# Two-layer conditioned trunk: another order inside the groups of seven products, and of the first loads, copies and splits

## The chip, the cores and the metric

The kernel runs on one core of a Trainium2 chip. The metric is device microseconds (us) of one execution. Engines are named as in the profile: PE is the matmul engine (PEld its weight loads), DVE the vector engine, ACT the scalar engine, POOL GpSimd, SP the engine that issues most DMAs.

## What is computed

The reference is a decoder trunk of two layers on 512 tokens of width 1024, in fp32. Each layer has three sub-layers, each with a normalisation that is scaled and shifted by values made from a conditioning vector c:

```python
cs = jax.nn.silu(c)
for l in range(DEPTH):
    mod = (cs @ ada_w[l] + ada_b[l])          # 3 sub-layers x (shift, scale, gate)
    h = _rmsnorm(x, norm_g[l, 0]) * (1.0 + mod[:, 0, 1]) + mod[:, 0, 0]
    x = x + 0.5 * mod[:, 0, 2] * _swiglu(h, ffn_w_gate[l, 0], ffn_w_up[l, 0], ffn_w_down[l, 0])
    h = _rmsnorm(x, norm_g[l, 1]) * (1.0 + mod[:, 1, 1]) + mod[:, 1, 0]
    x = x + mod[:, 1, 2] * _mixer(h, w_in[l], conv_w[l], w_conv_out[l], w_attn_out[l], w_o[l], rel_bias)
    h = _rmsnorm(x, norm_g[l, 2]) * (1.0 + mod[:, 2, 1]) + mod[:, 2, 0]
    x = x + 0.5 * mod[:, 2, 2] * _swiglu(h, ffn_w_gate[l, 1], ffn_w_up[l, 1], ffn_w_down[l, 1])
return _rmsnorm(x, final_g)
```

`_swiglu` is `(silu(h @ w_gate) * (h @ w_up)) @ w_down` with an inner width of 2816 (22 blocks of 128); `_mixer` is a short convolution beside dilated window attention. So there are four FFNs and two mixers, in the order FFN, mixer, FFN, FFN, mixer, FFN.

## The kernel before, in words

**Numbers.** Every matmul operand is split into a high and a low part (`A.copy` on ACT makes the high one, `sub`, L145, on DVE the low one), and each product is three matmuls: high x high, high x low, low x high. The activations stay transposed on chip: `xT` (the residual), and `hh` and `hl`, the two parts of the modulated, normalised input of a sub-layer, in eight blocks k of 128 features by 512 tokens.

**Where things lie.** Split operands lie in a pool R of 49 slots, fp32 scratch in a pool F of 19 slots (128x512 each). `Slots.take` hands out the first slot in the list of free ones; a slot that is given back goes to the list's end. Who takes a slot waits until its last readers are done. The PSUM banks have three tags: "mm" (4), "at" (2), "o" (2).

**An FFN.** Gate and up weights are multiplied in groups of two blocks of 128 columns (`m`, `m + 1`). One group is `seven`: a 2x2 block product by seven products instead of eight. a and c are the two halves of the gate weights (by input features), b and d those of the up weights. The products need a, c as loaded, or the differences a-b, a-d, b-d, c-a (L558, on DVE), against a quarter of `h` (`quarter`) or one of four sums of quarters (`Sums`, once for each FFN: four additions or subtractions of 128x1024 and four splits). Each product has 24 matmuls of 128x256. Its results are copied out of PSUM (`kept`, L554, on ACT) and added up (`plus`, L561, on DVE). After two or three groups the matching part of the down product runs (`down`, L214 splits its weights), and adds to `xT` (L373).

**Between sub-layers** stands `boundary`: `finish` computes the last part of the down product in two token halves; for each half the norm is summed up (`Norm`), and `modulated` makes `hh` and `hl` block by block: `t` = xT times the norm (L361, DVE), then `hh` (L362, ACT), an fp32 copy `u` (L366 on ACT for even k, L364 on POOL for odd k), then `hl` (L145, DVE). `t` lies in a slot that is taken and given back for each k. Behind each k stand 12 matmuls of 128x256, of the first four weight blocks of the next sub-layer.

**Modulation.** `modulation` loads 512 KB of `ada_t` for each k (SP), and multiplies and sums it against c on DVE (L297); these steps are spread over the products (`tick`). In the FFNs two loads are ahead, in the mixers one (`depth=1`).

**The start.** x is loaded and transposed by PE into PSUM, copied to `xT` (L1211 on ACT, L1213 on DVE), the first weights are split (L214; the first parts on POOL), c is loaded by ACT's queue, and the first FFN's `hh` and `hl` are made block by block while PE multiplies them (L1268).

**What sets the order.** The program is written as one sequence; a scheduler reorders the instructions of each engine by its own cost model, and each engine then works through its list in order, waiting at semaphores.

Of the kernel before, what the change touches and what calls it, by code (L numbers as in the profile page):

```python
# [27 lines left out]
ALU = mybir.AluOpType  # L28
# [18 lines left out]
N_R, N_LOW, N_F, RAWS = 49, 33, 19, 4  # L47
# [29 lines left out]
class Slots:  # L77
# [38 lines left out]
def trunk(ctx: ExitStack, tc: tile.TileContext, x, c, ada_t, ada_b, norm_g, ffn_w_gate, ffn_w_up, ffn_w_down,  # L116
# [196 lines left out]
    def modulation(l, s, j, depth=2):  # L313
# [10 lines left out]
        for k in range(depth):  # L324
            fetch(k)
        for k in range(NC):
            w = ahead.pop(0)
            weighted(m, k, w.ap)
            w.give()
            fetch(k + depth)  # L330
            yield
# [120 lines left out]
    def boundary(src, rhs, gate, l, s, units, whole=None):  # L452
# [14 lines left out]
        finish(src, rhs, gate, norms, hook)  # L467
        dsts = [bank("mm") for _ in units]
# [12 lines left out]
        return dsts  # L481
# [55 lines left out]
    def seven(raw1, raw2, sums, done):  # L537


        a, c = raw1[:, :4], raw1[:, 4:]  # L540
        b, d = raw2[:, :4], raw2[:, 4:]

        def run(*args):
            p = product(*args)
            next(p)
            return p

        def end(p):
            for _ in p:
                pass  # L550

        def kept(src):
            s = F.take()
            A.copy(s.ap, src)  # L554
            return s

        def minus(dst, x, y):
            V.tensor_tensor(dst, x, y, op=ALU.subtract)  # L558

        def plus(s, src):  # L560
            V.tensor_tensor(s.ap, s.ap, src, op=ALU.add)  # L561

        one = bank("mm")
        end(run(a, quarter(0, 0), one, True))
        p1 = kept(one)
        yield
        minus(a, b, a)
        three = bank("o")
        p = run(a, sums(1), three, True)
        minus(a, d, a)  # L570
        end(p)
        end(run(a, sums(2), one))
        u2 = kept(one)
        two = bank("at")
        end(run(c, quarter(1, 0), two, True))
        plus(p1, two)
        minus(b, d, b)
        end(run(b, sums(3), one))
        u3 = kept(one)
        plus(u3, three)  # L580
        yield
        minus(c, c, a)
        end(run(c, quarter(1, 1), one))
        end(run(d, sums(4), three))
        plus(u2, three)
        done(p1, u2, one, u3)

# [30 lines left out]
    def ffn(l, i, get, first, whole):  # L618

        acts = {}  # L620
        R.top = N_LOW
        sums = Sums(whole.ap.rearrange("p (k n) -> p k n", k=NC))
        whole.give()

# [10 lines left out]
        def swiglu_pair(m):  # L635
            def done(g1, u1, g2, u2):

                A.activation(g1.ap, g1.ap, AF.Silu)
                V.tensor_tensor(u1.ap, u1.ap, g1.ap, op=ALU.mult)
                g1.give()  # L640
                s = F.take()
                A.activation(s.ap, g2, AF.Silu)
                V.tensor_tensor(u2.ap, u2.ap, s.ap, op=ALU.mult)
                s.give()
                hi, lo = R.take(2), R.take(2)
                hv, lv = (s.ap.rearrange("p (c n) -> p c n", c=2) for s in (hi, lo))
                for half, t in enumerate((u1, u2)):
                    tv = t.ap.rearrange("p (c n) -> p c n", c=2)
                    A.copy(hv[:, :, HALF[half]], tv)  # L649
                    sub(lv[:, :, HALF[half]], tv, f(hv[:, :, HALF[half]]))  # L650
                    t.give()
                acts[m], acts[m + 1] = zip(hi.apart(), lo.apart())

            return done

        ahead = {}

        def begin(m):

            if m < DFF // P:  # L660
                ahead[m] = seven(*get.raws(m), sums, swiglu_pair(m))
                next(ahead[m])

        def up(part):
            modulating["share"] = SHARE_UP
            for m in range(*part):
                if m in acts:
                    continue
                if m < len(first) or m % 2:
                    if m < len(first):  # L670
                        pg, pu = first[m]
                    else:
                        g, u = get(m)
                        pg, pu = any_bank(), any_bank()
                        project([(pg, g)], h, NC)
                        project([(pu, u)], h, NC)
                    swiglu(m, pg, pu)
                    if m % 2 and m + 1 >= len(first):
                        begin(m + 1)
                    continue  # L680
                pair = ahead.pop(m)
                next(pair)
                begin(m + 2)
                for _ in pair:
                    pass
                if m + 2 == DFF // P:
                    sums.give()
# [478 lines left out]

    cs = F.take(2)
# [211 lines left out]
```

## Time and profile before

| what | us |
|---|---|
| median of 3 runs (2685.22 to 2687.23) | 2686.24 |
| the profiled execution | 2685.69 |
| its span, first to last instruction | 2683.9 |
| PE busy in it | 2620.5 (98%) |
| DVE busy | 1838.3 (68%) |
| ACT busy | 1171.6 (44%) |

The profiled execution is 0.55 us under the median. A matmul's row shows its own length; matmuls overlap, so what one costs is the distance from its start to the next one's. The mean granted clock of PE is 0.993 of full speed.

### The profile page before, as it was taken

Reading aid. Unit: us, or ns where it says so; the run is one execution under the profiler, and the core shown is the slowest. Engines: PE = TensorE matmul, PEld = TensorE weight load, DVE = VectorE, ACT = ScalarE, POOL = GpSimd, SP = SyncE. Lnnn points to the kernel's source line nnn. Section 1 sums busy time; section 2 is a strip of 40 time slices with the busy share of each in tenths; the row PEclk is TensorE's granted clock in tenths of the full one; section 3 lists DMA queues with packets and bytes.
Section 4 is the critical chain, followed back from the end, with each engine's and each line's share of the span. In section 5 each row is a group of like instructions: output and inputs, shape, how many; then the busy total and the mean of one; then the engine's idle time right before and its main releaser. Section 6 shows DMA issues by size and latency. Waiting matters only on the chain.

```text
span 2683.9 us, 40526 instructions
## 1 busy us (share of the span) xinstructions
PE 2620.5 (98%) x16265; PEld 2347.2 (87%) x16265; DVE 1838.3 (68%) x2874; ACT 1171.6 (44%) x2200; POOL 227.7 (8%) x551
## 2 busy tenths in 40 slices
PE   6899999999999999999999999999999999999999
PEld 5798999788888889989999999988888888989998
DVE  7996778888463358667787777885536534677675
ACT  4453454343353236434554444543443423544443
POOL 1000023121010001000020000330110000200001
PEclk8999999999999999999999999999999999999999
DMA  8732246767222231333224332562322322133321
GB/s 282 249 128 91 93 146 222 270 203 248 75 95 79 87 118 44 99 110 109 96 64 130 106 110 77 179 217 86 97 69 79 118 81 85 63 111 99 98 83 67
DMA packets 285480, 326.42 MB, mean 122 GB/s; under 512 B 8057, under 2 KB 263404, under 8 KB 285292
## 3 DMA queue, kind: packets, MB, share of 16 engines
q1 hardware_dynamic: 284836, 323.19, 36.8%
q8 instruction: 127, 2.08, 0.3%
q10 hardware_dynamic: 456, 0.65, 0.1%
q14 instruction: 61, 0.50, 0.1%
HBM read 321.67 MB, written 2.13 MB: 121 GB/s over the span
## 4 chain that ended last, share of the span: by engine, by line
PE 84%; DVE 9%; DMA 3%; ACT 3%; issue 1%; POOL 1%; DVEq 0%; POOLq 0%; SPq 0%; ACTq 0%
PE mm L531 16%; PE mm L234 12%; PE mm L235 12%; PE mm L236 12%; PE o L531 8%; PE at L531 4%; PE mm L1046 3%; DMA slots_f<-in_ada_t_dram 2%; DVE slots_f L297 2%; PE o L234 2%; PE o L236 2%; PE o L235 2%; PE at L236 2%; PE at L234 2%; PE at L235 2%; DVE slots_r L145 2%
## 5 line engine op out<-in xcount | busy, mean ns | idle before, releaser
L214 DVE TENSOR_TENSOR slots_r<-raw,slots_r 128x512 fp32r<-128x512 f32 (+2 forms) x578 | 361.0, 642 | 340.5 <-PE mm L235 162.1
L213 ACT CAST slots_r<-raw 128x512 fp32r<-128x512 f32 (+2 forms) x584 | 325.1, 582 | 403.2 <-PE mm L236 170.9
L234 PE MATMUL mm<-hh,slots_r 128*128 128x512 f32 (+1 forms) x1320 | 487.8, 370 | 0.0
L235 PE MATMUL mm<-hl,slots_r 128*128 128x512 f32 (+1 forms) x1320 | 483.0, 366 | 0.0
L236 PE MATMUL mm<-hh,slots_r 128*128 128x512 f32 (+1 forms) x1320 | 482.2, 365 | 0.0
L145 DVE TENSOR_TENSOR slots_r<-raw,slots_r 128x1024 fp32r<-128x1024 f32 (+3 forms) x401 | 379.9, 970 | 130.2 <-ACT slots_r L522 55.4
L522 ACT CAST slots_r<-raw 128x1024 fp32r<-128x1024 f32 x273 | 282.5, 1048 | 363.0 <-DVE raw L558 93.7
L236 PEld LDWEIGHTS mm<-hh,slots_r 128*128 128x128 f32 x1320 | 248.4, 188 | 43.3
L234 PEld LDWEIGHTS mm<-hh,slots_r 128*128 128x128 f32 x1320 | 248.9, 189 | 36.5
L235 PEld LDWEIGHTS mm<-hl,slots_r 128*128 128x128 f32 x1320 | 248.9, 189 | 36.1
L531 PE MATMUL mm<-slots_r 128*128 128x256 f32 x1872 | 240.6, 284 | 3.5 <-ACT slots_r L522 2.2
L531 PE MATMUL o<-slots_r 128*128 128x256 f32 x1872 | 236.3, 283 | 5.1 <-DVE slots_r L145 5.0
L531 PEld LDWEIGHTS o<-slots_r 128*128 128x128 f32 x1872 | 229.9, 191 | 8.1 <-DVE slots_r L145 6.2
L531 PEld LDWEIGHTS mm<-slots_r 128*128 128x128 f32 x1872 | 230.8, 191 | 6.4 <-ACT slots_r L522 2.8
L531 PE MATMUL mm<-hh,slots_r 128*128 128x256 f32 x1248 | 229.5, 280 | 2.7 <-DVE slots_r L145 1.3
L234 PE MATMUL mm<-slots_r 128*128 128x512 f32 (+1 forms) x584 | 212.3, 364 | 0.2 <-ACT slots_r L649 0.2
L235 PE MATMUL mm<-slots_r 128*128 128x512 f32 (+1 forms) x584 | 212.3, 364 | 0.0
L236 PE MATMUL mm<-slots_r 128*128 128x512 f32 (+1 forms) x584 | 212.1, 363 | 0.0
L297 DVE CUSTOM_DVE_ANT_0 slots_f<-slots_f 128x1024 f32<-128x1024 f32 x144 | 176.1, 1232 | 42.0 <-DMA slots_f<-in_ada_t_dram 41.0
L531 PEld LDWEIGHTS mm<-hh,slots_r 128*128 128x128 f32 x1248 | 193.7, 188 | 5.7 <-DVE slots_r L145 2.2
L558 DVE TENSOR_TENSOR raw<-raw 128x1024 f32<-128x1024 f32 x156 | 189.6, 1220 | 2.2
L531 PE MATMUL mm<-hl,slots_r 128*128 128x256 f32 x624 | 174.0, 279 | 0.0
(194 smaller groups left out, 4373.7 us busy)
## 6 DMA issues: line engine op xcount, KB each, us to landing
slots_f<-in_ada_t_dram SPq DMA_DIRECT2D x144, 512.0 KB, 4.5
raw<-in_w_in_dram SPq DMA_DIRECT2D x52, 1024.0 KB, 5.7
raw<-in_ffn_w_gate_dram SPq DMA_DIRECT2D x42, 1024.0 KB, 5.3
raw<-in_ffn_w_up_dram SPq DMA_DIRECT2D x42, 1024.0 KB, 6.2
raw<-in_ffn_w_down_dram SPq DMA_DIRECT2D x32, 768.0 KB, 4.3
raw<-in_w_in_dram SPq DMA_DIRECT2D x48, 512.0 KB, 5.3
raw<-in_ffn_w_down_dram SPq DMA_DIRECT2D x20, 512.0 KB, 3.5
raw<-in_w_conv_out_dram SPq DMA_DIRECT2D x8, 1024.0 KB, 4.8
```

The lines of the kernel that those rows point to most:

```text
L145: V.tensor_tensor(out_, a, b, op=ALU.subtract)
L213: A.copy(hv, src)
L214: (eng or V).tensor_tensor(lv, src, f(hv), op=ALU.subtract)
L234: T.matmul(dst, hi, xh[:, cols], start=first, stop=False)
L235: T.matmul(dst, hi, xl[:, cols], start=False, stop=False)
L236: T.matmul(dst, lo, xh[:, cols], start=False, stop=last)
L297: V.tensor_tensor_reduce(out=w, in0=w, in1=cs.ap, scale=1.0, scalar=0.0, op0=ALU.mult, op1=ALU.add, accum_out=m[:, k:k + 1])
L522: A.copy(hv, src)
L531: T.matmul(dst, a, b, start=first and k == i == n == 0, stop=True, skip_group_check=True)
L558: V.tensor_tensor(dst, x, y, op=ALU.subtract)
L1046: T.matmul(dst, a, b, start=k == 0 and r % 2 == 0 and n == 0, stop=True, skip_group_check=True)
```

## The change

1. `seven` becomes a class `Seven` that is driven step by step. Its first two products are now p1 (a times a quarter) and p2 (c times a quarter), which need no sums; they run between products of the group before (p1 between p6 and p7 of that group, p2 between p7 and p4). For the first group of the three later FFNs they run in the boundary ahead (`more`), p1 in an "o" bank, and `Sums` comes behind them; in the first FFN they run behind the product of its fourth weight block.
2. `modulation` has two loads ahead everywhere.
3. `Slots.take` prefers, for single slots and while fewer than 24 are free, a slot whose neighbour (`i ^ 1`) isn't free, so that pairs stay whole. R has 47 slots, F 21. F's last slot, 20, has no neighbour.
4. The start: c is loaded by SP behind the x loads, its SiLU stands behind the norm; all copies to `xT` and all the weight splits of the start are on DVE; the `ada_t` loads start one block earlier; a later block's weights are split earlier.

```diff
-N_R, N_LOW, N_F, RAWS = 49, 33, 19, 4
+N_R, N_LOW, N_F, RAWS = 47, 31, 21, 4
+AHEAD = 2
+SPARE = 12
...
-        for i in self.free:
-            if i + n <= self.top and all(i + j in self.free for j in range(n)):
-                return self.at(i, n)
-        raise ValueError("no slot is free")
+        ok = [i for i in self.free if i + n <= self.top and all(i + j in self.free for j in range(n))]
+        if n == 1 and len(ok) < 2 * SPARE:
+
+            ok.sort(key=lambda i: i ^ 1 in self.free)
+        if not ok:
+            raise ValueError("no slot is free")
+        return self.at(ok[0], n)
...
-    def modulation(l, s, j, depth=2):
+    def modulation(l, s, j):
...
-        for k in range(depth):
+        for k in range(AHEAD):
...
         finish(src, rhs, gate, norms, hook)
+        begun = more() if more else None
...
+            one, two, three = bank("o" if first else "mm"), bank("at"), bank("o")
+            p1 = begun(a, quarter(0, 0), one, True)
+            p2 = begun(c, quarter(1, 0), two, True)
+            yield
+            end(p1)
+            c11 = kept(one)
+            yield
+            end(p2)
+            plus(c11, two)
+            yield
+            minus(a, b, a)
+            p5 = begun(a, summed(1), three, True)
+            minus(a, d, a)
+            p6 = begun(a, summed(2), one)
+            end(p5)
+            end(p6)
+            c12 = kept(one)
+            yield
+            minus(b, d, b)
+            p7 = begun(b, summed(3), one)
+            end(p7)
+            c22 = kept(one)
+            plus(c22, three)
+            yield
+            minus(c, c, a)
+            p4 = begun(c, quarter(1, 1), one)
+            p3 = begun(d, summed(4), three)
+            end(p4)
+            end(p3)
+            plus(c12, three)
...
-    cs = F.take(2)
-    nc.scalar.dma_start(cs.ap, c.to_broadcast([P, D]))
...
+    cs = F.take(2)
+    nc.sync.dma_start(cs.ap, c.to_broadcast([P, D]))
...
-            if g:
-                A.copy(dst, src)
-            else:
-                V.tensor_copy(dst, src)
+            V.tensor_copy(dst, src)
...
     for u in units:
-        u.split(0, G)
+        u.split(0)
...
-        modulate(*((RATE_MIX, modulation(*a, depth=1)) for a in ahead if a not in ready))
+        modulate(*((RATE_MIX, modulation(*a)) for a in ahead if a not in ready))
```

Two places show how the instructions of an engine move. The first is DVE in the boundary between layer 0's mixer and its second FFN, second token half; `L361` (before) and `L366` (now) write `t`, `hl` is the low part. Before:

```order
L361 TENSOR_TENSOR slots_f<-xT,at 128x256 x5
L145 TENSOR_TENSOR hl<-slots_f,hh 128x256 x2
L361 TENSOR_TENSOR slots_f<-xT,at 128x256 x2
L145 TENSOR_TENSOR hl<-slots_f,hh 128x256 x2
L361 TENSOR_TENSOR slots_f<-xT,at 128x256
L145 TENSOR_TENSOR hl<-slots_f,hh 128x256 x4
```

Now, from the norm's last steps on:

```order
L349 SCALAR_TENSOR_TENSOR rs<-rs 128x2
L350 SCALAR_TENSOR_TENSOR rs<-rs 128x2
L150 TENSOR_TENSOR hl<-slots_f,hh 128x256
L366 TENSOR_TENSOR slots_f<-xT,at 128x256
L150 TENSOR_TENSOR hl<-slots_f,hh 128x256
```

The last two rows repeat: the two kinds alternate now, one k at a time, thirteen times in a row. The second place is DVE right behind the last of these `hl`, up to the second split that p6 waits for: sums of quarters (L495 to L501 before, L502 to L508 now), splits, the swiglu of the first two blocks (L628; L653 now), and the differences (L558; L576 now). Before:

```order
L495 TENSOR_TENSOR slots_f<-slots_f 128x4x256
L497 TENSOR_TENSOR slots_f<-slots_f 128x4x256
L145 TENSOR_TENSOR slots_r<-raw,slots_r 128x1024 x2
L558 TENSOR_TENSOR raw<-raw 128x1024 x2
L145 TENSOR_TENSOR slots_r<-slots_f,slots_r 128x1024 x2
L498 TENSOR_TENSOR slots_f<-slots_f 128x4x256
L628 TENSOR_TENSOR slots_f<-slots_f,mm 128x512 x2
```

Now:

```order
L502 TENSOR_TENSOR slots_f<-slots_f 128x4x256
L150 TENSOR_TENSOR slots_r<-raw,slots_r 128x1024
L504 TENSOR_TENSOR slots_f<-slots_f 128x4x256
L150 TENSOR_TENSOR slots_r<-slots_f,slots_r 128x1024
L579 TENSOR_TENSOR slots_f<-slots_f,at 128x512
L505 TENSOR_TENSOR slots_f<-slots_f 128x4x256
L150 TENSOR_TENSOR slots_r<-slots_f,slots_r 128x1024
L653 TENSOR_TENSOR slots_f<-slots_f,mm 128x512 x2
L150 TENSOR_TENSOR slots_r<-slots_f,slots_r 128x1024
L150 TENSOR_TENSOR slots_r<-slots_f,slots_r 128x512
L508 TENSOR_TENSOR slots_f<-slots_f 128x4x256
L150 TENSOR_TENSOR slots_r<-slots_f,slots_r 128x512
```

`L579`, the addition of p2's result, stands between the sums now; the difference that p6 uses (L576) follows behind the last row shown, and its split three rows later.

## Rows read from the trace of the kernel before

**Rows 1.** The page, busy time of each engine.

```profile
PE 2620.5 (98%) x16265; PEld 2347.2 (87%) x16265; DVE 1838.3 (68%) x2874; ACT 1171.6 (44%) x2200; POOL 227.7 (8%) x551
```

**Rows 2.** Stretches: length, then PE, PEld, DVE, ACT, POOL busy, PE clock, DMA.

```profile
100.00:350.00 250.00, 250.00 (x1730) 231.71 (x1730) 201.70 (x258) 109.40 (x155) 0.00 (x0) 1.00 0.39 128
...
425.00:700.00 275.00, 263.91 (x1454) 225.05 (x1453) 218.66 (x402) 110.88 (x287) 57.04 (x153) 0.99 0.66 217
...
990.00:1060.00 70.00, 65.74 (x544) 64.31 (x543) 55.16 (x91) 41.23 (x67) 14.23 (x20) 1.00 0.14 45
...
1370.00:1420.00 50.00, 47.76 (x397) 47.04 (x397) 47.16 (x63) 32.10 (x45) 4.38 (x7) 1.00 0.14 43
...
1690.00:1970.00 280.00, 278.92 (x1610) 242.73 (x1609) 194.54 (x370) 124.99 (x300) 62.00 (x157) 1.00 0.44 137
...
2310.00:2370.00 60.00, 54.89 (x440) 53.45 (x439) 49.34 (x77) 37.85 (x58) 10.29 (x15) 0.97 0.11 36
```

**Rows 3.** PE's waits in the whole run: total us, times, longest.

```profile
PE at L236 <- DVE slots_r L214: 6.8, 1, 6.8
PE o L884 <- DVE slots_r L145: 6.7, 6, 4.5
...
PE o L531 <- DVE slots_r L145: 5.0, 3, 3.3
```

**Rows 4.** Timeline of POOL and DVE in the start: start us, length.

```profile
14.37 1.22 DVE L297 CUSTOM_DVE_ANT_0 slots_f<-slots_f 128x1024 f32<-128x1024 f32 x1 [5.29 <-DMA slots_f<-in_ada_t_dram]
...
19.85 4.92 POOL L214 TENSOR_TENSOR slots_r<-raw,slots_r 128x512 fp32r<-128x512 f32 x4
...
19.91 1.22 DVE L343 TENSOR_TENSOR rs<-rs 128x4 f32<-128x4 f32 x1 [0.91 <-POOL rs L342]
...
63.78 0.69 DVE L145 TENSOR_TENSOR hl<-slots_f,hh 128x512 fp32r<-128x512 f32 x1 [1.59 <-ACT slots_f L1240]
```

**Rows 5.** Timeline of PE around the stall at 74 to 81 us.

```profile
73.11 0.39 PE L234 MATMUL mm<-hh,slots_r 128*128 128x512 f32 x1
73.33 0.39 PE L235 MATMUL mm<-hl,slots_r 128*128 128x512 f32 x1
...
81.20 0.79 PE L236 MATMUL at<-hh,slots_r 128*128 128x512 f32 x1 [6.78 <-DVE slots_r L214]
...
82.22 0.63 PE L235 MATMUL at<-hl,slots_r 128*128 128x512 f32 x1
82.65 0.63 PE L236 MATMUL at<-hh,slots_r 128*128 128x512 f32 x1
```

**Rows 6.** Timeline of PE in a steady stretch, matmuls of a product.

```profile
149.86 0.28 PE L531 MATMUL at<-hl,slots_r 128*128 128x256 f32 x1
149.98 0.28 PE L531 MATMUL at<-hh,slots_r 128*128 128x256 f32 x1
```

**Rows 7.** DVE's waits, 400 to 700 us; PE's timeline; the page's DMA issues.

```profile
DVE slots_f L297 <- DMA slots_f<-in_ada_t_dram: 27.7, 20, 3.4
...
486.10 1.44 PE L884 MATMUL o<-slots_r 128*128 128x256 f32 x5 [4.47 <-DVE slots_r L145]
...
slots_f<-in_ada_t_dram SPq DMA_DIRECT2D x144, 512.0 KB, 4.5
```

**Rows 8.** Timeline of DVE in the boundary before the second FFN.

```profile
1014.79 0.41 DVE L361 TENSOR_TENSOR slots_f<-xT,at 128x256 f32<-128x256 f32 x1
...
1016.42 1.74 DVE L361 TENSOR_TENSOR slots_f<-xT,at 128x256 f32<-128x256 f32 x5
...
1018.07 0.95 DVE L145 TENSOR_TENSOR hl<-slots_f,hh 128x256 fp32r<-128x256 f32 x2
...
1023.45 1.23 DVE L495 TENSOR_TENSOR slots_f<-slots_f 128x1024 f32<-128x1024 f32 x1
```

**Rows 9.** Timeline of DVE behind it, and all copies of L554 (min/median/max).

```profile
1030.93 2.48 DVE L558 TENSOR_TENSOR raw<-raw 128x1024 f32<-128x1024 f32 x2
...
L554 ACT COPY slots_f<-mm x117: 573/585/592, 91.6 to 2631.8; 128x512 f32<-128x512 f32 x117
```

More of the change, by code (lines that the diff above doesn't have):

```diff
@@ L535, in product @@
         lo.give()
[L537 to L586, printed above, removed]
@@ new lines, in trunk, with __init__, go, run @@
+    class Seven:
+        def __init__(self, raw1, raw2, first=False):
+            self.sums, self.out = None, None
+            self.steps = self.run(raw1, raw2, first)
+            self.go()
+        def go(self, n=1):
+            for _ in range(n):
+                next(self.steps, None)
+        def run(self, raw1, raw2, first):
+            a, c = raw1[:, :4], raw1[:, 4:]
+            b, d = raw2[:, :4], raw2[:, 4:]
+            def begun(*args):
+                p = product(*args)
+                next(p)
+                return p
+            def end(p):
+                for _ in p:
+                    pass
+            def kept(src):
+                s = F.take()
+                A.copy(s.ap, src)
+                return s
+            def minus(dst, x, y):
+                V.tensor_tensor(dst, x, y, op=ALU.subtract)
+            def plus(s, src):
+                V.tensor_tensor(s.ap, s.ap, src, op=ALU.add)
+            def summed(i):
+                return lambda k: self.sums(i)(k)
+            one, two, three = bank("o" if first else "mm"), bank("at"), bank("o")
[28 more added lines that the diff above has]
+            plus(c12, three)
+            self.out = c11, c12, one, c22
@@ L633, in swiglu @@
             acts[m] = hi, lo
[L635 to L662, printed above, removed]
+        def swiglu_pair(m, g1, u1, g2, u2):
+            A.activation(g1.ap, g1.ap, AF.Silu)
+            V.tensor_tensor(u1.ap, u1.ap, g1.ap, op=ALU.mult)
+            g1.give()
+            s = F.take()
+            A.activation(s.ap, g2, AF.Silu)
+            V.tensor_tensor(u2.ap, u2.ap, s.ap, op=ALU.mult)
+            s.give()
+            hi, lo = R.take(2), R.take(2)
+            hv, lv = (s.ap.rearrange("p (c n) -> p c n", c=2) for s in (hi, lo))
+            for half, t in enumerate((u1, u2)):
+                tv = t.ap.rearrange("p (c n) -> p c n", c=2)
+                A.copy(hv[:, :, HALF[half]], tv)
+                sub(lv[:, :, HALF[half]], tv, f(hv[:, :, HALF[half]]))
+                t.give()
+            acts[m], acts[m + 1] = zip(hi.apart(), lo.apart())
@@ new lines, in begin @@
+        def begin():
+            sums = Sums(whole.ap.rearrange("p (k n) -> p k n", k=NC))
+            whole.give()
+            return sums
+        modulating["share"] = SHARE_UP
+        if len(first) % 2:
+            sums = begin()
+            for m, banks in enumerate(first):
+                swiglu(m, *banks)
+            m = len(first)
+            banks = [any_bank() for _ in range(2)]
+            for pd, u in zip(banks, get(m)):
+                project([(pd, u)], h, NC)
+            swiglu(m, *banks)
+            group.go(2)
+        else:
+            group.go(2)
+            sums = begin()
+            for m, banks in enumerate(first):
+                swiglu(m, *banks)
@@ L664, in up @@
+        group.sums = sums
+        groups = {len(acts): group}
         def up(part):
@@ L668, in up @@
                     continue
-                if m < len(first) or m % 2:
-                    if m < len(first):
-                        pg, pu = first[m]
-                    else:
[L673 to L686, printed above, removed]
+                here, after = groups.pop(m), None
+                here.go()
+                if m + 2 < DFF // P:
+                    after = groups[m + 2] = Seven(*get.raws(m + 2))
+                    after.sums = sums
+                    after.go()
+                here.go()
+                if after:
+                    after.go()
+                here.go()
+                swiglu_pair(m, *here.out)
+                if not after:
                     sums.give()
@@ L1316, in trunk @@
             whole, wv = unsplit()
-            banks = boundary(src, rhs, gate, l + 1, 0, [u for m in range(2) for u in get(m)], wv)
+            banks, group = boundary(src, rhs, gate, l + 1, 0, [u for m in range(2) for u in get(m)], wv,
+                                    lambda: begin_group(get))
             give()
```

44 lines of the change are left out of this document (25 added, 19 removed).

## The prediction, made before the changed kernel ran

> **What bounds the kernel now.** I read the page first: PE is busy for 2620.5 of 2683.9 us [rows 1], so all that can be won is its 63 us of idle time and what it loses at a lower clock; the change moves work and adds none on PE. Next came the table of stretches [rows 2], which tells where that idle time lies. The stretch at 100 to 350 us, groups and down products, has none: PE busy 250 of 250. The first mixer (425 to 700) lacks 275 - 263.9 = 11.1 us; the second one (1690 to 1970) 1.1. The starts of the three later FFNs lack 70 - 65.7 = 4.3, 50 - 47.8 = 2.2 and 60 - 54.9 = 5.1. The list of PE's waits [rows 3] names the first FFN's start too: one wait of 6.8 us for DVE. Last I read timelines of DVE, ACT and PE at these places [rows 4 to 9]. The reader is to see that PE is always behind DVE where it waits, that DVE is fully used only at the starts, and that a steady group costs PE no wait at all.
>
> Prices: a matmul of 256 columns 149.98 - 149.86 = 0.12 us [rows 6], so a product of 24 takes 2.85; one of 512 columns 0.22 to 0.23, and 0.43 behind the long stall [rows 5]; a DVE operation of 128x1024 1.24 [rows 9], 1.14 from start to start in a row.
>
> **The change, part by part.**
>
> *The start and the first group: -5.5.* DVE's norm step L343 takes 1.22 us, as long as one of the POOL splits that it starts beside (four in 4.92) [rows 4]; L344 and L345 go the same way. With the splits on DVE that wait goes, and the four x copies that ACT made move to DVE. I walked DVE's new order with these durations: PE's first product starts some 4 us earlier, DVE's last `hl` comes at about 61 instead of 64.5, and the first block's matmuls end some 2.0 us earlier. Then p1 and p2 (5.7 us of PE) lie where DVE makes the sums. So the 6.8 us wait goes, and with it 12 matmuls at 0.43 instead of 0.23 (2.4 us) [rows 5]. But the difference and split that p5 needs come behind the sums in DVE's order, and I find waits of some 5.7 us at p5 and p6. 2.0 + 6.8 + 2.4 - 5.7 = 5.5. Bounds: -9 (no wait at p5), -2 (the start wins nothing, and the waits are 1.5 longer). c's load goes behind x; the first L297 waited 5.29 us for `ada_t` and not for c [rows 4], so this cover is gone only if c lands over a microsecond later than the loads of x, which the lower bound holds.
>
> *Two modulation loads ahead in the mixers: -8.* In the first mixer DVE waits 20 times, 27.7 us in all, for `ada_t`, whose 512 KB land 4.5 us after the issue [rows 7]. One such wait stands ahead of the split for which PE sat idle 4.47 us at 486. In the second mixer, where PE lacks only 1.1 us [rows 2], such waits are few. So 11.1 - 1.1 = 10 us of PE hang on it, and some lower clock (0.99 in that stretch), which I put at the 1.8 us of the third start (0.03 of 60 us) [rows 2]. The new order has three slots in turn instead of two, but some of the first loads wait for slots that PE or POOL reads: I take 8. Bounds: 0 (the slots come no sooner) and -11.8.
>
> *The three FFN starts in boundaries: +15.* Here lies my main term, and it is on the slot rule. `modulated` takes and gives back `t` for each k. With fewer than 24 slots in F (it has 21) the new rule is always on, and slot 20 has no neighbour, so it is preferred as often as it is free: `t` is slot 20 in each of the last 14 of 16 steps. L366 for the next k must then wait for `hl` of this one. Before, up to five L361 ran ahead [rows 8], and ACT worked through them without a gap. The order shows the new alternation (first place shown above). What a step costs when nothing runs ahead, the trace has once: from L361 at 1014.79 to the next at 1016.42, 1.63 us (odd k). For an even k I take L361 at 1016.42 to `hl` at 1018.07 plus 0.34 to DVE's next start [rows 8]: 1.99. Mean 1.81; thirteen such steps take 23.5 us from about 1014, so `hl` is complete at about 1037, where it was at 1023.4 (L495 follows at 1023.45 [rows 8]).
>
> PE itself doesn't feel this in the boundary: 12 matmuls for each k take 1.42 us, and p1 and p2 fill the rest, so that p2 ends at about 1040, as it would with no wait at all. What is late is DVE. Behind the last `hl` it has now four sums, their splits, a swiglu, the difference for p6 and three splits (second place shown): 12 operations at 1.14, five at 0.6, with L579 among them, which waits for p2: about 17 us. p5 starts at +4.8 us after the last `hl`, but p6 at +14.7 to +17, while PE has nothing from +8. Waits of 1.3 + 6.6 + 1.1 + 0.5 = 9.5 us. DVE did the like before while PE was 11 us behind it. Against the waits that the three places have now [rows 2]: 9.5 - 4.3, 9.5 - 2.2, 9.5 - 5.1, in sum 16.9; less 1.8 us of lower clock at the third (0.97 in that stretch): 15.1. Bounds: -5 (DVE gets the difference done inside the chain's gaps, and the waits of before go in part), and +20 (each 6.6 us wait also lowers the clock, by 1.8 to 2.4 us, as behind the stall of 6.78 [rows 5]).
>
> *The two boundaries ahead of mixers: +4.* The same alternation, but no p1. 14 steps of 1.81 are 25.3 us against 14 x 1.42 = 19.9 of PE, into which the order puts some twenty 512-column matmuls of the mixer (4.6). The first block waits some 2 us more. 2 each; bounds 0 and 8.
>
> *Slots and banks in the steady stretches: +8.* The same rule hands out a slot that was just given back where the list's head was the oldest. In the order I looked for splits and copies that wait for a matmul, and counted the matmuls from there to the one that needs the result. Where these are fewer than the operation takes (copy 0.585 [rows 9], 0.16 for the last matmul to end, 0.1 for two handovers), PE waits. Before, 10 places fall short, by 2 us in all; now 53, by 14: sixteen copies of L572 with 0 to 7 matmuls behind them in the same bank, the splits of down weights, four of group weights. Some 4 of the 12 more lie at the starts, counted above. Bounds 2 (DVE and ACT come early after all) and 12.
>
> p1, p6, p7 and p4 of a group share one bank, before as now, and the stretch of 250 us without a wait [rows 2] shows that the copies between them cost nothing while another product lies between. Now it is p1 and p2 of the next group that lie there, save in each FFN's last group. Were each of the 117 copies exposed, at some 0.8 us, the sum would be 90 us higher; that stretch gives this no chance. [...]
>
> *At nothing:* pools of 47 and 21, the extra bank, six more splits on DVE in the start (in the walk), one DMA moved to SP.
>
> **The sum:** 2685.7 - 5.5 - 8 + 15.1 + 4 + 8 = 2699.3; that execution is 0.55 us under the median, well inside what can be told. I say 2699. No change means within 0.2%, 5.4 us of 2686.2, about what a measurement can tell.
>
> **The rivals.**
>
> *Faster: the fill works as written.* p1 and p2 are 5.7 us that need no sums at each start; if DVE makes the difference for p6 in the gaps of the chain (1.81 less its two operations of 0.4 leave it 1 us idle in each step), the starts cost nothing more than before and the steady places 2: 2685.7 - 5.5 - 8 + 0 + 1 + 3 = 2676. It decides from a chain that ends before 1030. For it: that idle time. Against: the list is in order, and no such work stands there. Chance 0.2.
>
> *No change: gains and losses of one size.* Starts +7, boundaries +2, steady +5: 2686. For it: each 9.5 is a walk by hand. Chance 0.2.
>
> *Loads stay late.* The two loads ahead are issued in order by SP behind slots that come free late, and the first mixer wins nothing: 2699 + 8 = 2707. For it: some loads now wait for PE. Chance 0.1.
>
> *The clock falls at each start.* Three waits of over 6 us, each followed by 2 us of half clock as at 81 us [rows 5]: 2699 + 6 = 2705. Against: the waits come in pieces, and behind the 3.3 us wait at the second FFN the clock stayed at 1.00 [rows 2, 3]. The Trainium skill, "TensorE: Matmul & The Clock Gate", section "HAM oscillation", tells the same: a long enough gap throttles PE, and each gap pays again. Chance 0.12.
>
> **How the numbers follow.** Forecast 0.38, rivals 0.2, 0.2, 0.1, 0.12. Slower is 0.38 + 0.1 + 0.12 = 0.6, same 0.2, faster 0.2. The range goes from the first rival, 2676, to 2716 (the last two together, 2713, and 3 for the upper bound of a term).
>
> **What would show it.** Right: DVE alternates L366 and L150 with ACT idle between, the last `hl` of the second FFN's start at about 1033 to 1040, counted by the sums behind it, a PE wait of 5 us or more at p6 in each of the three boundaries, DVE's waits for `ada_t` in the first mixer under 10 us, small waits of PE for L572 and L218 in the stretch that had none. Wrong: PE idle at the three starts under 12 us in sum, or the loads' waits unchanged.

## The result: 2.2% slower, and the profile after

The changed kernel took 2744.86 us (median of 4 runs, 2744.53 to 2751.28) against 2686.73 (4 runs, 2685.22 to 2688.7): a ratio of 1.0222, 95% interval 1.0204 to 1.0239. The forecast was 2699, and the range ended at 2716: the sign held, the size did not. The profiled execution of the changed kernel has a span of 2743.0 us and a mean granted clock of 0.989 (0.993 before).

The page of the changed kernel, busy time of each engine:

```profile
PE 2657.5 (97%) x16265; PEld 2359.7 (86%) x16265; DVE 1839.8 (67%) x2884; ACT 1182.5 (43%) x2196; POOL 236.0 (9%) x545
```

Against [rows 1] the work is the same: 16265 matmuls, DVE and ACT within 11 us. PE's *busy* time grew by 37 of the 59 us, so its idle times show 22 us of the loss. The Trainium skill, "Perfetto Trace Analysis", section "Identifying the Most-Contended Engine", says that matmul busy time is a poor measure of how close PE is to its limit, since matmuls are pipelined, and names the share of the weight loads as one of two better ones. The trace agrees: the weight loads' busy time grew by 12.5 us only, and their share fell from 87 to 86%. A short wait is larger than its row says: at 1534.88 us the row names 0.76 us of idle time, while PE's two starts around it lie 1.04 us apart, where 0.12 is the price. So I measured from landmarks, the first norm matmul of each boundary (L396 before, L401 now), in both traces, and from each matmul's start to the next one's.

| stretch between landmarks, us | before | after | difference |
|---|---|---|---|
| first FFN | 386.5 | 387.5 | +1.0 |
| boundary and first mixer | 614.4 | 621.8 | +7.4 |
| boundary and second FFN | 357.3 | 363.2 | +5.9 |
| boundary and third FFN | 351.5 | 372.8 | +21.3 |
| boundary and second mixer | 598.6 | 609.8 | +11.2 |
| boundary and fourth FFN | 356.0 | 368.6 | +12.6 |
| end | 19.6 | 19.3 | -0.3 |

The loss is spread over the whole run; no single place holds it. The stretches of the changed kernel, columns as in [rows 2]:

```profile
100.00:350.00 250.00, 246.24 (x1667) 224.81 (x1666) 191.13 (x245) 106.23 (x150) 0.00 (x0) 1.00 0.35 117
430.00:700.00 270.00, 262.02 (x1441) 222.49 (x1440) 218.80 (x400) 109.19 (x284) 55.99 (x152) 1.00 0.67 223
1045.00:1080.00 35.00, 27.24 (x209) 26.54 (x208) 32.81 (x34) 20.78 (x26) 0.00 (x0) 0.90 0.19 61
1370.00:1440.00 70.00, 59.26 (x453) 57.60 (x451) 48.68 (x79) 35.37 (x57) 13.14 (x17) 0.90 0.11 36
...
2370.00:2430.00 60.00, 54.02 (x424) 52.86 (x423) 47.40 (x64) 35.54 (x50) 5.28 (x6) 0.94 0.11 36
```

Steady groups that had not one wait now lack 3.76 us of 250, and 1667 matmuls lie there instead of 1730. Compared by PE's starts at the same matmul number, the changed kernel is 9.8 us ahead at 145 us and 1.0 behind at the first landmark, so this part of the first FFN costs 10.8 us more. The starts of the second and third FFN lack 7.8 and 10.7 us, and the clock fell there to a mean of 0.90. The first mixer still lacks 8 us. PE's waits of the whole run (total us, times, longest):

```profile
PE o L538 <- DVE slots_r L150: 16.8, 9, 7.7
PE o L538 <- ACT slots_r L529: 12.2, 6, 6.3
...
PE o L916 <- DVE slots_r L150: 5.4, 8, 2.5
...
PE mm L240 <- DVE hl L150: 4.2, 9, 2.0
PE at L401 <- POOL slots_f L392: 3.8, 3, 1.6
...
PE mm L538 <- ACT slots_f L572: 2.0, 4, 0.7
```

The 6.8 us of the first FFN [rows 3] are gone; waits of the products in bank "o" for their operands (L150, L529) took their place, 29 us in all where DVE's part was 5.0.

**The start of the second FFN.** DVE from the first `hl` of the second token half to the split that p6 waits for:

```profile
1021.93 0.42 DVE L150 TENSOR_TENSOR hl<-slots_f,hh 128x256 fp32r<-128x256 f32 x1
1022.27 0.41 DVE L366 TENSOR_TENSOR slots_f<-xT,at 128x256 f32<-128x256 f32 x1
1023.42 0.42 DVE L150 TENSOR_TENSOR hl<-slots_f,hh 128x256 fp32r<-128x256 f32 x1 [0.74 <-POOL slots_f L369]
1023.76 0.41 DVE L366 TENSOR_TENSOR slots_f<-xT,at 128x256 f32<-128x256 f32 x1
1025.34 0.42 DVE L150 TENSOR_TENSOR hl<-slots_f,hh 128x256 fp32r<-128x256 f32 x1 [1.16 <-ACT slots_f L371]
...
1044.70 0.43 DVE L150 TENSOR_TENSOR hl<-slots_f,hh 128x256 fp32r<-128x256 f32 x1 [1.53 <-ACT hh L367]
1045.16 1.23 DVE L502 TENSOR_TENSOR slots_f<-slots_f 128x1024 f32<-128x1024 f32 x1
...
1057.25 1.21 DVE L576 TENSOR_TENSOR raw<-raw 128x1024 f32<-128x1024 f32 x1
1058.38 1.21 DVE L150 TENSOR_TENSOR slots_r<-slots_f,slots_r 128x1024 fp32r<-128x1024 f32 x1
```

And PE behind it, at p5 (bank "o", 23 of its matmuls), at the first matmuls of p6, and just behind them:

```profile
1049.85 3.02 PE L538 MATMUL o<-slots_r 128*128 128x256 f32 x23 [1.10 <-DVE slots_r L150]
...
1059.59 0.80 PE L538 MATMUL o<-slots_r 128*128 128x256 f32 x2 [6.26 <-ACT slots_r L529]
...
1061.38 0.41 PE L538 MATMUL mm<-hl,slots_r 128*128 128x256 f32 x1
1061.60 0.63 PE L538 MATMUL mm<-hh,slots_r 128*128 128x256 f32 x2
```

The chain is the one forecast, one L366 and one L150 at a time, DVE idle in each step. Compare [rows 8], where five L361 stand in a row. From the first of these `hl` to the last it takes 1044.70 - 1021.93 = 22.8 us, 8 us later than forecast, since the boundary itself begins 8.4 later (1009.3 against 1000.9). The sums follow at 1045.16. Counted from the end of the last `hl`, p5 goes on 4.7 us later (its first matmul had not needed the late split) and p6 starts 14.5 later, after a wait of 6.26. The matmuls behind that wait start 0.22 us apart, as in the last two rows, where 0.12 is the price: half clock (1.2 of 2.4 GHz).

**A steady group.** ACT near 230 us:

```profile
229.53 1.05 ACT L529 CAST slots_r<-raw 128x1024 fp32r<-128x1024 f32 x1 [2.08 <-PE at L240]
233.84 2.94 ACT L529 CAST slots_r<-raw 128x1024 fp32r<-128x1024 f32 x3 [3.26 <-PE at L241]
```

DVE there:

```profile
232.55 1.23 DVE L150 TENSOR_TENSOR slots_r<-raw,slots_r 128x1024 fp32r<-128x1024 f32 x1 [4.43 <-PE at L241]
```

PE, at the first product that reads these splits:

```profile
236.83 0.50 PE L538 MATMUL o<-slots_r 128*128 128x256 f32 x2 [1.39 <-ACT slots_r L529]
```

Here the splits of the next group's weights wait 3.26 us (ACT) and 4.43 us (DVE) for a matmul of the down product, which still reads the slots that they were given. Two more casts stand behind the first on ACT; then PE, done with the down product, waits 1.39 us for the last of the three. ACT and DVE had time enough before, and lost it standing behind PE.

### The profile page after: what moved, and what is told of

It reads as the page before. It is cut to its first block, busy times and chain, and to the rows that moved or that the text cites. A ratio compares the mean times of both kernels' runs of the same rounds, so it can differ in the third digit from the quotient of the medians.

```text
span 2743.0 us, 40527 instructions
## 1 busy us (share of the span) xinstructions
PE 2657.5 (97%) x16265; PEld 2359.7 (86%) x16265; DVE 1839.8 (67%) x2884; ACT 1182.5 (43%) x2196; POOL 236.0 (9%) x545
## 4 chain that ended last, share of the span: by engine, by line
PE 51%; DVE 6%; DMA 2%; ACT 1%; issue 1%; POOL 1%; DVEq 0%; POOLq 0%; ACTq 0%; SPq 0%
PE mm L538 10%; PE mm L239 7%; PE mm L240 7%; PE mm L241 7%; PE o L538 6%; PE at L538 2%; DVE slots_r L150 2%; PE mm L1078 2%; PE o L239 1%; PE o L241 1%; PE o L240 1%; PE at L239 1%; PE at L240 1%; PE at L241 1%; PE o L916 1%
## 5 line engine op out<-in xcount | busy, mean ns | idle before, releaser
L219 DVE TENSOR_TENSOR slots_r<-raw,slots_r 128x512 fp32r<-128x512 f32 (+2 forms) x584 | 368.5, 647 | 372.7 <-PE mm L240 167.6
L218 ACT CAST slots_r<-raw 128x512 fp32r<-128x512 f32 (+2 forms) x584 | 330.6, 582 | 601.2 <-PE mm L241 211.7
L240 PE MATMUL mm<-hl,slots_r 128*128 128x512 f32 (+1 forms) x1320 | 479.1, 369 | 4.5 <-DVE hl L150 4.2
L241 PE MATMUL mm<-hh,slots_r 128*128 128x512 f32 (+1 forms) x1320 | 476.6, 367 | 0.8 <-DVE slots_r L219 0.6
L239 PE MATMUL mm<-hh,slots_r 128*128 128x512 f32 (+1 forms) x1320 | 458.1, 371 | 0.0
L150 DVE TENSOR_TENSOR slots_r<-raw,slots_r 128x1024 fp32r<-128x1024 f32 (+3 forms) x401 | 378.4, 970 | 85.3 <-ACT slots_r L529 51.6
L529 ACT CAST slots_r<-raw 128x1024 fp32r<-128x1024 f32 x273 | 280.6, 1047 | 234.9 <-DVE raw L576 71.1
L538 PE MATMUL o<-slots_r 128*128 128x256 f32 x2016 | 268.0, 288 | 29.1 <-DVE slots_r L150 16.8
L240 PEld LDWEIGHTS mm<-hl,slots_r 128*128 128x128 f32 x1320 | 249.5, 189 | 47.2 <-DVE hl L150 9.6
L241 PEld LDWEIGHTS mm<-hh,slots_r 128*128 128x128 f32 x1320 | 249.3, 189 | 45.3 <-DVE slots_r L219 2.7
L538 PEld LDWEIGHTS o<-slots_r 128*128 128x128 f32 x2016 | 255.8, 196 | 35.7 <-DVE slots_r L150 19.7
L239 PEld LDWEIGHTS mm<-hh,slots_r 128*128 128x128 f32 x1320 | 236.0, 189 | 38.4 <-ACT hh L367 0.9
L538 PE MATMUL mm<-slots_r 128*128 128x256 f32 x1728 | 229.9, 286 | 6.3 <-DVE slots_r L150 3.9
L538 PEld LDWEIGHTS mm<-slots_r 128*128 128x128 f32 x1728 | 215.9, 192 | 12.6 <-DVE slots_r L150 6.0
L538 PE MATMUL mm<-hh,slots_r 128*128 128x256 f32 x1152 | 219.0, 282 | 2.3 <-DVE slots_r L150 0.9
L240 PE MATMUL mm<-slots_r 128*128 128x512 f32 (+1 forms) x584 | 212.3, 364 | 0.0
L576 DVE TENSOR_TENSOR raw<-raw 128x1024 f32<-128x1024 f32 x156 | 189.9, 1219 | 10.3 <-DMA raw<-in_ffn_w_up_dram 8.5
L538 PEld LDWEIGHTS mm<-hh,slots_r 128*128 128x128 f32 x1152 | 181.8, 189 | 6.1 <-ACT slots_f L572 2.9
L538 PE MATMUL mm<-hl,slots_r 128*128 128x256 f32 x576 | 161.0, 280 | 0.0
```

The source lines that it names most:

```text
L150: V.tensor_tensor(out_, a, b, op=ALU.subtract)
L218: A.copy(hv, src)
L219: (eng or V).tensor_tensor(lv, src, f(hv), op=ALU.subtract)
L239: T.matmul(dst, hi, xh[:, cols], start=first, stop=False)
L240: T.matmul(dst, hi, xl[:, cols], start=False, stop=False)
L241: T.matmul(dst, lo, xh[:, cols], start=False, stop=last)
```

## The experiments

Two theories stood after the result. **A**: the slot rule makes all of the loss, through `t` in F and through hot slots in R, and the rest of the change gains. **B**: the new order of products and the smaller pool R have a share in it. Each run is compared with runs of the kernel before on its own chip, whose medians were 2690.08, 2689.83, 2688.47 and 2688.85. A single run carries a few us of spread: runs of one kernel on one chip lay up to 11 us apart.

**1. The change without the slot rule, old pool sizes.** With slots handed out in order of age the pool of 47 has no free pair at some point, so the sizes go back too.

```diff
-N_R, N_LOW, N_F, RAWS = 47, 31, 21, 4
+N_R, N_LOW, N_F, RAWS = 49, 33, 19, 4
...
-SPARE = 12
+SPARE = 0
```

> The changed kernel with the old slot rule and the old pool sizes (49, 33, 19); the order of the products, the loads ahead and the start stay new. Theory A (the slot rule: it hands out slots that were just given back, so that t, copies and splits wait for their last readers) gives 2670 to 2692: the waits at the starts, in the boundaries and in the steady stretches go. Theory B (the order of the products: p1 and p2 ahead need their splits earlier, and five products in a row then need all of DVE's differences) gives 2725 or more, with PE still idle 15 us or more at the three starts. Theory C (both, half each) lies between, about 2705.

Measured: 2663.44 (2661.42 to 2667.98), ratio 0.991 (0.9885 to 0.9934). Repeated later:

> The changed kernel with the old slot rule and sizes once more, beside the next one on the same chip: 2660 to 2668.

It gave 2665.59 (2661.96 to 2669.11), 0.9907 (0.9887 to 0.9927). The first result lies below A's range, far from B's. The same places of this kernel, same columns:

```profile
100.00:350.00 250.00, 250.00 (x1719) 230.88 (x1719) 197.29 (x256) 108.95 (x157) 0.00 (x0) 1.00 0.42 132
960.00:1060.00 100.00, 99.41 (x756) 95.55 (x755) 80.97 (x133) 55.51 (x96) 14.86 (x20) 1.00 0.23 72
1340.00:1400.00 60.00, 59.42 (x487) 58.94 (x486) 51.59 (x81) 37.22 (x59) 11.51 (x16) 0.97 0.12 36
2270.00:2340.00 70.00, 69.32 (x540) 66.92 (x539) 53.45 (x97) 38.71 (x70) 15.81 (x20) 1.00 0.16 52
```

The three starts lack 0.6, 0.6 and 0.7 us, less than before the change [rows 2] (4.3, 2.2, 5.1): p1 and p2 do fill them. What stood in the way was the rule, which costs some 81 us here (runs 3 and 4 show that the pool sizes, also undone, have no part in it).

**2. The slot rule alone, in the kernel before.**

```diff
-        for i in self.free:
...
+        ok = [i for i in self.free if i + n <= self.top and all(i + j in self.free for j in range(n))]
+        if n == 1 and len(ok) < 24:
+            ok.sort(key=lambda i: i ^ 1 in self.free)
...
```

> The kernel before with the new slot rule and nothing else (pools 49 and 19). Theory A: slower than before by 25 to 50 us, with a boundary chain of 1.8 us for each k. Theory B: within 6 us of before, 2686.

Measured in one run: 2773.24, +83, far above A's own 25 to 50. So rule alone +83, rest alone -27 (run 1 against its own before), and both together +58: the parts add up to within 2 us, and B falls. PE's longest waits there stand at the same kinds of place:

```profile
PE mm L533 <- ACT slots_f L556: 11.4, 13, 3.5
PE mm L237 <- DVE hl L147: 9.7, 20, 1.2
```

**3 to 6. Which pool, and which takers.** First the rule in R alone, F by age (sizes 47, 21):

```diff
-        if n == 1 and len(ok) < 2 * SPARE:
+        if n == 1 and self.whole and len(ok) < 2 * SPARE:
...
-    R = Slots(const.tile([P, N_R, S], F32R, name="slots_r"), N_R)
+    R = Slots(const.tile([P, N_R, S], F32R, name="slots_r"), N_R, True)
```

> The changed kernel with the new slot rule for pool R alone; pool F takes the oldest free slot again (sizes 47 and 21 kept). Theory A says that t no longer lies in one slot: DVE runs several L367 ahead again, the last hl of the second FFN's start comes near 1030, and the waits of the three starts and of the mixers' boundaries (some 35 us against before) shrink to 10, while the steady stretches keep their 30: 2715 to 2722. Theory B: within 8 us of 2745, since the chain of t was filled by p1 and p2.

Measured: 2702.0, so F's share is 43, and A's 2715 to 2722 had it too small. The same with the old sizes (`N_R, N_LOW, N_F, RAWS = 49, 33, 19, 4`):

> The changed kernel with the new slot rule for pool R alone, and the old sizes (49, 33, 19). If it is the rule that makes the splits wait for slots that the down product still reads: 2695 to 2705, as with 47 slots (2702). If it is the smaller pool (two slots fewer for the groups): 2663 to 2675, as with the rule undone in both (2663).

2704.19: the sizes are worth nothing that can be told, and the other half of the loss, some 40 us, is the rule in R. Then one taker alone goes by age, the `t` of `modulated`, all else as changed (`oldest` takes the first slot in the list):

```diff
-        t = F.take()
+        t = F.oldest()
```

> The changed kernel with one edit: the t of modulated takes the oldest free slot of F; all other single slots keep the new rule. Theory A1 (of what the rule costs in pool F, 43 us by the run with F's rule undone, the serial t is nearly all, through the starts and the boundaries): 2700 to 2712, the last hl of the second FFN's start at about 1030 and no PE wait over 3 us in the three boundaries. Theory A2 (the copies of products and the swiglu's slots in F matter as much): 2720 to 2735.

2704.51: `t` alone is 40 of F's 43. Last, `t` and the weight splits of `Unit.split`, old sizes:

```diff
-                hi, lo = R.take(), R.take()
+                hi, lo = R.oldest(), R.oldest()
```

> The changed kernel with the sizes 49, 33, 19, where t and the two slots of each weight split of 128x512 (L218, L219: down products and the mixers) take the oldest free slot; all other single slots keep the new rule. Theory A3 (in pool R the rule costs through these splits, which got slots given back 1 to 3 takes before): 2663 to 2675. Theory A4 (it costs through other users, pairs for the products or the mixers' probabilities): 2690 or more.

2668.74, 5 and 3 us above run 1's two medians: two takers, `t` and the weight splits, carry nearly all of it. By the landmarks of these traces (after less run 3; run 3 less run 1; run 1 less before), from the first stretch of the table above to the sixth: the rule in F +0.4, +1.8, +9.8, +11.2, +10.0, +10.0; in R +7.7, +9.2, +3.2, +11.1, -0.2, +9.2; the rest -7.1, -3.6, -7.1, -1.0, +1.4, -6.6. With `t` alone undone (after less its run) the same stretches give -0.1, +1.7, +10.3, +12.6, +6.9, +9.0: `t` costs 7 to 13 us in each of the four later stretches, one of them a mixer's. Where the rule in R costs is not settled: with the old sizes (run 4 less run 1) it is +7.8, +4.9, +15.7, +5.5, 0.0, +8.7, so the sizes move the loss from place to place, though not its sum.

**7. Two loads ahead in the mixers, alone, in the kernel before.**

```diff
-        modulate(*((RATE_MIX, modulation(*a, depth=1)) for a in ahead if a not in ready))
+        modulate(*((RATE_MIX, modulation(*a)) for a in ahead if a not in ready))
```

> The kernel before with two modulation loads ahead in the mixers and nothing else. The forecast of the prediction, 8 us from DVE's waits for ada_t in the first mixer, gives 2678, with these waits under 10 us. The rival (the waits were hidden or come back at other places) gives 2684 to 2690.

2685.62 against 2683.03 to 2694.27: nothing that can be told in the whole. DVE's waits for `ada_t` fell to 22.0 us, not under 10:

```profile
DVE slots_f L297 <- DMA slots_f<-in_ada_t_dram: 22.0, 21, 2.3
```

By landmarks the first mixer took 610.3 us instead of 614.4, and the two FFNs behind it 1.7 and 1.3 more. PE's timeline where [rows 7] has the wait of 4.47, and a place 75 us later:

```profile
484.44 0.87 PE L884 MATMUL o<-slots_r 128*128 128x256 f32 x5 [2.65 <-DVE slots_r L145]
...
561.92 0.72 PE L860 MATMUL at<-ident,slots_f 128*128 128x128 f32 x2 [1.88 <-ACT slots_f L853]
```

The first wait is 1.8 shorter, and another of 1.88 stands behind it. The stretch around the first (columns as in [rows 2]):

```profile
462.00:490.00 28.00, 25.35 (x160) 22.80 (x159) 23.27 (x44) 9.26 (x21) 8.12 (x17) 0.94 0.98 317
```

The DMA engines are busy 0.98 of it, where they were 0.82 before, and a load there lands 4.2 us after its issue (median) instead of 3.3. I read this as a second load that stands in line rather than arrives early; no run takes the weight loads beside it away. The reverse, run 1 with one load ahead in the mixers (`depth=1`):

> The changed kernel with the old slot rule and sizes, and one load ahead in the mixers as before. If the second load ahead is worth little to PE (as the run of it alone says, about 1 us): 2662 to 2666. If it needs the other changes to pay, as the prediction's 8 us would have it: 2668 to 2672.

2668.85 in one run, 4 above the mean of run 1's two medians: in the range of the prediction's 8 us, but no more than the spread. By PE's starts its first mixer takes 4.6 us more than run 1's.

**8. The new start alone, in the kernel before** (c by SP, its SiLU behind the norm, copies and splits on DVE, `ada_t` a block earlier):

```diff
-            if g:
-                A.copy(dst, src)
-            else:
-                V.tensor_copy(dst, src)
+            V.tensor_copy(dst, src)
...
-        u.split(0, G)
+        u.split(0)
...
-        if k + 3 < NC:
-            ada_load(k + 3)
+        elif k == 3:
+            g2[1].split()
+            u2[1].split(0)
```

> The kernel before with the new start alone (c behind x on SP, copies and splits on DVE, earlier loads and splits). By the prediction's sum 2.0 us from the earlier products and nothing else: 2684. If the start's gain doesn't need p1 and p2 there (the splits of the fourth block's weights are early now, so the 6.8 us wait goes anyway): 2674 to 2678. If moving work to DVE only shifts the wait: 2686 or more.

2680.72, 9 under its one run of before and between the ranges that were expected. The reverse, run 1 with the start of before (the same hunks undone):

> The changed kernel with the old slot rule and sizes and the old start (c on ACT's queue, splits partly on POOL, later loads and splits). If the start gives what it gave alone (6 to 9 us): 2669 to 2673, and the order of the products and the second load together 13 to 17 us against before. If start and product order share one gain (the 6.8 us wait): 2664 to 2668.

2691.94, outside both ranges: 28 worse than run 1, and not at the start alone; against run 1, 1175 to 1350 us holds 1119 matmuls instead of 1223. A different start shifts which slot everybody gets later. That is only argued from the place of the loss; the next runs test whether the loss hangs on the slot rule, not which slots collide.

**9. Another rule for slots.** Pairs go by the age of their younger half; a single slot prefers one whose neighbour is taken only within the older half of the list, and otherwise takes the oldest:

```diff
-        if n == 1 and len(ok) < 2 * SPARE:
-            ok.sort(key=lambda i: i ^ 1 in self.free)
+        if n > 1:
+            ok.sort(key=lambda i: max(self.free.index(i + j) for j in range(n)))
+        elif True:
+            old = [i for i in ok[:len(ok) // 2] if i ^ 1 not in self.free]
+            ok = old or ok
```

> The same with a rule that keeps pairs whole and looks at age: a pair whose later-freed half has been free longest; a single slot with a taken neighbour only from the older half of the free list, else the oldest. If what costs is a slot's age alone, it is no slower than the plain one, 2655 to 2668, since its pairs are older (the youngest tenth 10 takes against 7). If any preference costs, 2675 or more.

In the changed kernel with the old sizes: **2656.26** (2653.17 to 2659.95), ratio 0.9875 (0.9858 to 0.9891), below both kernels. With the start of before:

> The changed kernel with sizes 49, 33, 19, the rule by age (2656 with the new start) and the old start. If the 28 us of the old start under the oldest-slot rule were the history of the slots: 2661 to 2667. If they are the start's own: 2680 or more.

2661.43 (2658.75 to 2664.39), 0.9902 (0.9885 to 0.9918). So under this rule the start is worth 5 us, and the 28 above were not its own. In the kernel before, this rule alone:

> The kernel before with the rule by age and nothing else. If the oldest-slot rule already cost nothing there (no waits in its steady stretches): 2683 to 2690, and the change without its slot rule is worth 27 to 34. If pairs with one hot slot cost in the kernel before too: 2675 to 2682.

2668.77 (2666.1 to 2671.64), 0.9928 (0.9909 to 0.9947): 20 us out of the kernel before by the choice of slots alone, better than either range had it. And with one load ahead in the mixers:

> The changed kernel with sizes 49, 33, 19, the rule by age and one load ahead in the mixers. The second load was worth 1 us alone and about 5 in the changed kernel without the slot rule: 2658 to 2664; by the prediction's term of 8 us: 2664.

2652.8 (2651.74 to 2660.13), 0.9875 (0.9856 to 0.9894), below the range: the second load gains nothing here. From 2668.77 to 2661.43, 7 us, is left for the order of the products and the loads together.

In the program's own sequence I counted, for each weight split's slot, how many other takes from the pool lie between its last giving back and this take: with the new rule in R the youngest tenth has 3 or fewer (median 26), by age 14 (median 23), with the rule of run 9 12. The median says nothing; the youngest tenth tells the new rule from the two others. It does not order those two, 14 and 12, where run 9 is the faster; for the pairs of slots it does, 7 by age against 10 (the expectation of run 9). That the pairs make the difference is not shown by a run of its own.

## Why the prediction was right in sign and wrong in size

By PE's starts at the same matmul number in both traces, the terms came out as: start -9.8 (forecast -5.5), three FFN starts +20.6 (+15.1), two mixer boundaries +13.9 (+4), first mixer -3.2 up to 700 us (-8), three steady stretches +31 (+8), and +6.4 in the first mixer behind 700 us, which no term held. The other stretches, -1.3 to +1.7, nearly cancel; in sum the 59 us.

- *The three FFN starts, +15.1.* Right in mechanism and nearly in size: `t` alternates, a step takes 1.92 us for even k and 1.49 for odd (1.99 and 1.63 forecast), p5 4.7 us behind the last `hl` (4.8) and p6 14.5 (14.7 at least), p6's wait 6.26 (6.6). The three places cost 5.5, 12.8 and 2.3 us more, 20.6 in all, just above the upper bound, in which the clock falls behind each wait. It fell at all three (0.90, 0.90 and 0.94 in the stretches above), though the fourth FFN has two waits under 3 us where one of 5 or more was forecast. PE at the third FFN and at the fourth:

```profile
1422.19 4.97 PE L538 MATMUL o<-slots_r 128*128 128x256 f32 x24 [7.67 <-DVE slots_r L150]
...
2403.96 0.50 PE L538 MATMUL o<-slots_r 128*128 128x256 f32 x2 [2.88 <-ACT slots_r L529]
2407.05 5.07 PE L538 MATMUL o<-slots_r 128*128 128x256 f32 x22 [2.58 <-DVE slots_r L150]
```

- *Slots and banks in the steady stretches, +8.* **This is the step that failed most.** Three stretches alone (145 us to the first landmark, the third FFN behind its start, the end of the fourth) cost 10.8, 10.0 and 10.3, some 31. I counted single hops, one split or copy that waits for a matmul against the matmuls ahead of its reader, "53, by 14", with only four of them splits of group weights. But each engine works through its list in order. At 229 to 237 us the casts of a group's weights wait for PE, two more queue behind them, DVE's split of the same weights waits for PE as well, and the product in bank "o" pays at the end. From 1440 to 1740 us PE's waits name the splits of the products' operands (L150, L529) for 4.2 of 5.1 us, the copies of L572 for 0.9. Run 6 shows that the weight splits' slots are at the root: with these by age too, 36 us go (2704.51 to 2668.74). That the delay is handed on in this way at every such place is argued from the one shown.
- *The two mixer boundaries, +4.* They cost 4.2 and 9.7. I saw the wait for `hl` (L240, 4.2 us in all), but not that the norm comes later too: L401 waits 3.8 us for its squares (L396 waited 2.5 before) and L356 2.3 for the norm's result (L351 0.5), and the clock in the second fell to 0.91 from 1760 to 1780 us. That the squares' slots were just given back is the likely reason, not a tested one.
- *Two modulation loads ahead, -8.* Too large. DVE's waits for `ada_t` fell, as forecast:

```profile
DVE slots_f L302 <- DMA slots_f<-in_ada_t_dram: 9.4, 10, 2.3
```

  They are 9.4 us instead of 27.7 [rows 7]. But the loads alone bring them to 22.0 only (run 7), run 1 has 18.6, and the slot rule alone, with one load ahead, 17.6 (run 2). They fall where the kernel gets slower too, so they do not measure the load ahead. What failed is the step from the 10 us by which PE lacks more in the first mixer than in the second to waits for `ada_t`, and from one more load ahead to loads that land early enough. The kernel of run 9 has two ahead and still the long wait, 4.20 us of PE at 478, for the split in the last row here (SP, then DVE):

```profile
468.41 0.53 SPq L328 DMA_DIRECT2D slots_f<-in_ada_t_dram  x1
...
476.13 1.23 DVE L304 CUSTOM_DVE_ANT_0 slots_f<-slots_f 128x1024 f32<-128x1024 f32 x1 [3.69 <-DMA slots_f<-in_ada_t_dram]
477.28 0.08 DVE L304 DVE_READ_ACCUMULATOR2_ANT mod<- 128x1 f32 x1
477.28 0.69 DVE L152 TENSOR_TENSOR slots_r<-at,slots_r 128x512 fp32r<-128x512 f32 x1
```

  The semaphores of the trace tie this DVE step to the load that SP issued at 468.41, ahead of its use by 7.7 us, through which the DMA engines were busy 0.93. So it was not issued late, as the rival "loads stay late" has it; it took long to land, which agrees with the full engines of run 7. By PE's starts the second load gives the first mixer 4.1 us in the kernel before and 4.6 in run 1, and costs 2.6 in that of run 9; in the time of the whole kernel none of the three differences, 3.5 to 4.5 us, is clear of the spread.
- *The start, -5.5.* It gave 9.8 to the first group, past the lower bound of -9; run 8 shows 9 alone in one run, 5 under the rule of run 9. The norm's steps on DVE take 0.16 us each instead of 1.2 [rows 4], and PE's first product starts at 20.96 us instead of 27.77 (6.8 earlier, 4 forecast). PE's waits from 80 to 100 us, at p2 and at the products with the sums, come to 2.5 us instead of the 5.7 forecast at p5 and p6.
- *The reading of the rows.* "PE is always behind DVE where it waits" was not so: before the change PE also waited for ACT, 5.3 us for `hh` in the start and 3.5 for the casts of group weights (L522). Those casts, L529 now, make 12.2 us in bank "o" alone.
- *The rivals.* "Faster: the fill works as written" gave 2676 (its sum takes 3 for the steady places where its text says 2) and was put out by the wait for `t`. Without the rule the same order makes 2663: the mechanism was right, and the condition (a chain that ends early) was what the rule took away. In run 1 the sums start at 1011.63, 21 us behind the first norm matmul at 990.2; in the changed kernel 36 behind it. "The clock falls" came on top, at three starts: at 0.12 us each, the 24 and 22 matmuls of the rows above would have taken 2.9 and 2.6 us, so I estimate its price at some 2 us for each. The Trainium skill, "TensorE: Matmul & The Clock Gate", section "HAM oscillation", has each long gap throttle PE anew; by the 6.26 and 7.67 us waits the trace agrees (clock 0.90 in both stretches).
- *The range* ended at 2716, since each term was bounded by the places that the order showed to be short. Nothing in it stood for delay that one place passes on to the next.

## What to carry to other kernels

A rule that picks a buffer decides which instruction waits for which; between "the oldest free" and "one just given back" lay 83 us of 2690 here, with the same work and the same number of buffers. Judge such a rule by its youngest reuses, of pairs as well as of single slots, not by the median, and follow a late buffer through every queue that works in order behind it: here a cast that waited 3.26 us for PE held two casts behind it, and PE then waited 1.39 us for the last. And test a change of several parts by switching each one off in both kernels: here three parts gained 27 us, and the fourth, there to make room, cost 83.

## What was not expected

Of the 59 us that the run grew by, 37 stand in the profile as busy time of PE, at the same number of matmuls; whoever adds up idle times sees 22. And repeated bubbles came with free buffers at hand: the Trainium skill, "Perfetto Trace Analysis", section "Optimization Strategy", reads consistent bubbles as a possible lack of space for the next tile. Here 47 or 49 slots made no difference that can be told (2702.0 and 2704.19, one run each), and the choice among the free ones made nearly all of it. Also, an edit of the first 90 us (run 1 against its reverse in 8) moved 28 us under one rule and 5 under another.
